# Contrast adjustment of 48 image planes: the first tile of four planes is split into tiles of one, one and two planes

## The chip, the cores and the metric

The kernel runs on one NeuronCore of a Trainium2 chip. The metric is the device time of one execution in microseconds (us); lower is better. A core has a tensor engine (PE), a vector engine (DVE), a scalar engine (ACT), a GpSimd engine (POOL) and a sync engine (SP). Each runs its own instruction stream in order, and they wait for each other through semaphores. Data moves between DRAM and the on-chip memory through 16 DMA engines that serve two queues here: one filled by SP (loads), one filled by ACT (stores).

## The reference

```python
def setup_inputs():
    batch, c, h, w = 16, 3, 512, 512
    return {
        "x": np.random.rand(batch, c, h, w).astype(np.float32),
        "factor": np.float32(1.5),
    }

def reference(x: np.ndarray, factor: np.float32) -> np.ndarray:
    mean = np.mean(x, axis=(2, 3), keepdims=True)
    return np.clip(mean + factor * (x - mean), 0, 1).astype(np.float32)
```

There are 16 x 3 = 48 planes of 512 x 512 float32 numbers, 1 MB each; this document calls one plane an image. Each image needs its own mean before any of its numbers can be written. 50.33 MB are read and 50.33 MB are written. Written out, the result is clip(factor * x + (1 - factor) * mean, 0, 1).

## The kernel before

The images lie one behind the other in DRAM. A tile is 128 partitions by 8192 numbers (a row of 32 KB in each partition), 4 MB, which is exactly four images with 32 partitions each. There are 12 tiles, and a ring of six tile slots in on-chip memory, in which each tile is loaded, changed in place, and stored from.

For each tile `compute` (L78) does this:

1. DVE adds up columns 0 to 4351 of each partition (L81), while ACT adds up columns 4352 to 8191 through an activation with an accumulator (L84). The split is the constant SUM.
2. PE multiplies the two columns of partial sums with a 128 x 128 block matrix `blockw` (L86 for ACT's sums, L87 for DVE's). Its blocks of 32 x 32 hold (1 - factor) / (512 * 512), so that every partition of an image gets (1 - factor) * mean in `bias`. POOL writes the matrix at the start (L61, L63).
3. DVE computes factor * x + bias in place (L91), then clips with max and min in place (L94).
4. ACT issues the store (L101), behind DVE's clip.

The order of the work is written by hand. ACT runs its sum of tile t+1 behind the store of tile t in its stream, so it can't begin that sum before DVE has clipped tile t. SP issues the loads (L76): first the first 2048 columns of tile 0 (8 KB rows), then the other 6144 columns of tile 0 (24 KB rows), then tile 1, then tiles 2 and 3 in one DMA, then tiles 4 and 5 in one DMA. This fills the ring. From then on the load of tile t + 6 stands behind compute of tile t, and SP waits for the store of tile t before it issues it, since it goes to the same slot. Tile 0 is also finished and stored in two parts, of 2048 and of 6144 columns (FIRST, L89): two stores, with 8 KB and with 24 KB rows. A load of two tiles counts as landed only when both are there.

A DMA of 128 rows is cut into packets, one for each row, so that each of the 16 engines moves 8 packets of it.

Of the kernel before, what the change touches and what calls it, by code (L numbers as in the profile page):

```python
# [1 line left out]

# [4 lines left out]


P = 128  # L10
ROW = 8192
BUFS = 6
SHORT = 2048
FIRST = (SHORT, ROW - SHORT)
SUM = 4352


@with_exitstack
def kernel(
    ctx: ExitStack,  # L20
    tc: tile.TileContext,
    x: bass.AP,
    factor: float,
    out: bass.AP,
):

    nc = tc.nc
    f32 = mybir.dt.float32  # L30
    Alu = mybir.AluOpType
    Act = mybir.ActivationFunctionType

    B, C, H, W = x.shape
    n_img, n_pix = B * C, H * W
    ppi = n_pix // ROW
    per_tile = P // ppi
    n_tiles = n_img // per_tile
    assert ppi * ROW == n_pix and per_tile * n_tiles == n_img

    factor = float(factor)
    wconst = (1.0 - factor) / float(n_pix)

    x_f = x.rearrange("b c h w -> (b c h w)")
    out_f = out.rearrange("b c h w -> (b c h w)")

    def dram(ap, t, c0=0, c1=ROW):
        return bass.AP(tensor=ap.tensor, offset=t * P * ROW + c0, ap=[[ROW, P], [1, c1 - c0]])

    consts = ctx.enter_context(tc.tile_pool(name="consts", bufs=1))  # L50
    xpool = ctx.enter_context(tc.tile_pool(name="xpool", bufs=1))
    small = ctx.enter_context(tc.tile_pool(name="small", bufs=1))
    psum = ctx.enter_context(tc.tile_pool(name="psum", bufs=1, space=bass.MemoryType.PSUM))


    sums = small.tile([P, 2 * n_tiles], f32, name="sums")
    junk = small.tile([P, ROW - SUM], f32, name="junk")
    bias = psum.tile([P, n_tiles], f32, name="bias")

    blockw = consts.tile([P, P], f32, name="blockw")  # L60
    nc.gpsimd.memset(blockw, 0.0)  # L61
    for a in range(0, P, ppi):
        nc.gpsimd.memset(blockw[a : a + ppi, a : a + ppi], wconst)  # L63


    ring = xpool.tile([P, BUFS, ROW], f32, name="ring")

    def load(t, c0=0, c1=ROW, n=1):

        b = t % BUFS  # L70
        src = bass.AP(
            tensor=x_f.tensor,
            offset=t * P * ROW + c0,
            ap=[[ROW, P], [P * ROW, n], [1, c1 - c0]],
        )
        nc.sync.dma_start(out=ring[:, b : b + n, c0:c1], in_=src)  # L76

    def compute(t):  # L78
        xt = ring[:, t % BUFS, :]
        own = sums[:, 2 * t : 2 * t + 2]  # L80
        nc.vector.tensor_reduce(  # L81
            out=own[:, 0:1], in_=xt[:, 0:SUM], axis=mybir.AxisListType.X, op=Alu.add
        )
        nc.scalar.activation(out=junk, in_=xt[:, SUM:ROW], func=Act.Copy, accum_out=own[:, 1:2])  # L84
        shift = bias[:, t : t + 1]
        nc.tensor.matmul(shift, blockw, own[:, 1:2], start=True, stop=False)  # L86
        nc.tensor.matmul(shift, blockw, own[:, 0:1], start=False, stop=True)  # L87
        c = 0
        for n in FIRST if t == 0 else [ROW]:  # L89
            part = xt[:, c : c + n]  # L90
            nc.vector.tensor_scalar(  # L91
                out=part, in0=part, scalar1=factor, scalar2=shift, op0=Alu.mult, op1=Alu.add
            )
            nc.vector.tensor_scalar(  # L94
                out=part, in0=part, scalar1=0.0, scalar2=1.0, op0=Alu.max, op1=Alu.min
            )
            store(t, c, c + n)
            c += n

    def store(t, c0, c1):  # L100
        nc.scalar.dma_start(out=dram(out_f, t, c0, c1), in_=ring[:, t % BUFS, c0:c1])  # L101

    with tc.manual_schedule():
        load(0, c1=SHORT)
        load(0, c0=SHORT)
        load(1)
        load(2, n=2)
        load(4, n=2)
        for t in range(n_tiles):
            compute(t)  # L110
            if t + BUFS < n_tiles:
                load(t + BUFS)


# [1 line left out]
_INS = ['x', 'factor']  # L116
_OUTS = [((16, 3, 512, 512), 'float32')]

_NUMBERS = {'factor': 1.5}


# [26 lines left out]
```

## Time and profile before

| What | us |
|---|---|
| median of 3 runs | 239.27 (239.14 to 239.34) |
| span of the profiled execution, first to last instruction | 237.3 |
| DVE busy | 163.1 (69%) |
| ACT busy | 43.2 (18%) |
| PE busy | 14.1 (6%) |
| POOL busy | 0.9 |
| DVE sum of a tile, L81, 12 times | 4.683 each |
| ACT sum of a tile, L84, 12 times | 3.403 each |
| DVE scale and shift, 8192 columns, L91, 11 times | 4.491 each |
| DVE clip, 8192 columns, L94, 11 times | 4.427 each |
| DVE scale and shift, 2048 columns, L91, once | 1.291 |
| DVE clip, 2048 columns, L94, once | 1.227 |
| DVE idle in front of L81, waiting for loads | 45.7 in total |
| first load (1 MB), issue to landing | 4.8 |
| store of a tile, issue to landing, median | 35.8 |

The profile is of one execution; its own time on record is its span, and the runs' median includes what lies around it. The profile's page lists busy time by engine, cuts the span into 40 equal slices of about 5.9 us with the busy share of each engine and of the DMA engines in tenths, gives packets and bytes of each DMA queue with the time that their packets took as a share of all 16 engines, follows the chain of waits back from the end, and groups instructions by line. Other views give busy times and DMA traffic in chosen windows, the instructions in order of time, and the waits of each engine. q1 is the queue of SP's loads, q10 the queue of ACT's stores. In a window, packets are counted where they begin, so a share can come out somewhat over 100%.

DVE begins its first sum at 12.96 us, when the whole of tile 0 has landed. The first store is issued at 20.91 us, the last at 218.17 us. SP issues its first load at 0.74 us.

### The profile page before, as it was taken

What the parts mean: (1) busy time and instruction counts of PE and PEld (TensorE: products, weight loads), DVE (VectorE), ACT (ScalarE), POOL (GpSimd) and SP (SyncE); (2) the same over time, 40 slices, a digit from 0 to 9 for tenths busy, and PEclk for the clock granted to TensorE, in tenths of its full rate; (3) what the DMA queues carried; (4) which work ended last, traced back from release to release, by engine and by line L of the source; (5) the groups of instructions that cost most, each with busy time, mean ns of one, the idle gap of its engine ahead of it and who ended that gap; (6) DMA issues with size and microseconds to landing.
All of it is one profiled execution on the core that took longest, in us unless ns stands there. A gap on an engine that the chain in (4) does not pass through costs nothing.

```text
span 237.3 us, 285 instructions
## 1 busy us (share of the span) xinstructions
PE 14.1 (6%) x48; PEld 12.0 (5%) x48; DVE 163.1 (69%) x38; ACT 43.2 (18%) x25; POOL 0.9 (0%) x9
## 2 busy tenths in 40 slices
PE   0010010001010001010010100100100100010000
PEld 0010010001010001010010100100100100010000
DVE  0079989048989328999989898891892795687000
ACT  2050230041050023050320504101400500500000
POOL 1000000000000000000000000000000000000000
DMA  7999999999999999999999999999999999999996
GB/s 297 410 442 442 421 442 359 456 439 441 442 436 414 403 431 442 442 442 442 436 442 436 414 409 425 442 442 442 442 436 442 436 420 403 425 442 442 442 442 265
DMA packets 3712, 100.66 MB, mean 424 GB/s; under 512 B 384, under 2 KB 384, under 8 KB 384
## 3 DMA queue, kind: packets, MB, share of 16 engines
q1 hardware_dynamic: 1840, 50.33, 49.7%
q10 hardware_dynamic: 1872, 50.33, 49.2%
HBM read 50.33 MB, written 50.33 MB: 424 GB/s over the span
## 4 chain that ended last, share of the span: by engine, by line
DMA 57%; DVE 29%; another core or an unknown queue 3%; PE 1%; SPq 1%; issue 0%; DVEq 0%
DMA ring<-in_x_dram 41%; DMA out_dram<-ring 16%; DVE sums L81 10%; DVE ring L91 9%; DVE ring L94 9%; PE bias L87 1%; SPq L76 1%; DVEq L91 0%
## 5 line engine op out<-in xcount | busy, mean ns | idle before, releaser
L81 DVE TENSOR_REDUCE sums<-ring 128x1 f32<-128x4352 f32 x12 | 56.2, 4683 | 45.7 <-DMA ring<-in_x_dram 45.7
L84 ACT ACTIVATE junk<-ring 128x3840 f32<-128x3840 f32 x12 | 40.8, 3403 | 163.3 <-DMA ring<-in_x_dram 107.5
L91 DVE TENSOR_SCALAR ring<-ring,bias 128x8192 f32<-128x8192 f32 (+2 forms) x13 | 54.1, 4163 | 8.9 <-PE bias L87 7.4
L94 DVE TENSOR_SCALAR ring<-ring 128x8192 f32<-128x8192 f32 (+2 forms) x13 | 53.3, 4099 | 0.4
L86 PE MATMUL bias<-sums,blockw 128*128 128x1 f32 x24 | 7.0, 361 | 190.8 <-ACT junk L84 190.8
L86 PEld LDWEIGHTS bias<-sums,blockw 128*128 128x128 f32 x24 | 6.0, 312 | 191.7 <-ACT junk L84 175.2
L87 PE MATMUL bias<-sums,blockw 128*128 128x1 f32 x24 | 7.0, 363 | 4.3 <-DVE sums L81 3.9
L87 PEld LDWEIGHTS bias<-sums,blockw 128*128 128x128 f32 x24 | 6.0, 311 | 5.3 <-DVE sums L81 5.0
L84 ACT ACTIVATION_READ_ACCUMULATOR junk<-ring 128x1 f32 x12 | 2.2, 186 | 0.0
L84 ACT ACT_TABLE_LOAD x1 | 1.3, 1283 | 0.7 <-PEq L129 0.7
L63 POOL MEMSET blockw<- 32x32 f32 x4 | 0.5, 117 | 0.2
L61 POOL MEMSET blockw<- 128x128 f32 x1 | 0.2, 204 | 0.3 <-POOLq L129 0.3
L129 POOL MEMSET const-bfloat16-1.0<- 128x1 bf16 x1 | 0.1, 111 | 0.0
L129 POOL MEMSET const-uint8-127<- 128x1 uint8 x1 | 0.1, 111 | 0.0
L129 POOL MEMSET const-float32-1.0<- 128x1 f32 x1 | 0.1, 108 | 0.0
L129 POOL MEMSET const-float32-0.0<- 128x1 f32 x1 | 0.1, 103 | 0.2 <-issue 0.2
## 6 DMA issues: line engine op xcount, KB each, us to landing
out_dram<-ring ACTq DMA_DIRECT2D x11, 4096.0 KB, 35.8
ring<-in_x_dram SPq DMA_DIRECT2D x7, 4096.0 KB, 49.7
ring<-in_x_dram SPq DMA_DIRECT2D x2, 8192.0 KB, 66.7
ring<-in_x_dram SPq DMA_DIRECT2D x1, 3072.0 KB, 11.7
out_dram<-ring ACTq DMA_DIRECT2D x1, 3072.0 KB, 28.2
ring<-in_x_dram SPq DMA_DIRECT2D x1, 1024.0 KB, 4.8
out_dram<-ring ACTq DMA_DIRECT2D x1, 1024.0 KB, 17.5
```

The costliest lines, as they stand in the source:

```text
L61: nc.gpsimd.memset(blockw, 0.0)
L63: nc.gpsimd.memset(blockw[a : a + ppi, a : a + ppi], wconst)
L76: nc.sync.dma_start(out=ring[:, b : b + n, c0:c1], in_=src)
L81: nc.vector.tensor_reduce(out=own[:, 0:1], in_=xt[:, 0:SUM], axis=mybir.AxisListType.X, op=Alu.add)
L84: nc.scalar.activation(out=junk, in_=xt[:, SUM:ROW], func=Act.Copy, accum_out=own[:, 1:2])
L86: nc.tensor.matmul(shift, blockw, own[:, 1:2], start=True, stop=False)
L87: nc.tensor.matmul(shift, blockw, own[:, 0:1], start=False, stop=True)
L91: nc.vector.tensor_scalar(out=part, in0=part, scalar1=factor, scalar2=shift, op0=Alu.mult, op1=Alu.add)
L94: nc.vector.tensor_scalar(out=part, in0=part, scalar1=0.0, scalar2=1.0, op0=Alu.max, op1=Alu.min)
L129: nc = _bacc.Bacc("TRN2", target_bir_lowering=False, num_devices=1)
```

## The change

The first tile of four images becomes three tiles: image 0 alone, image 1 alone, and images 2 and 3 together. A tile of n images now has 128 / n partitions for each image, so that a tile of one image has 128 rows of 2048 numbers (8 KB), a tile of two has rows of 16 KB, and a tile of four has rows of 32 KB as before. The other eleven tiles hold the same images in the same rows as before. There are 14 tiles:

- Each tile is one load (alone, or two tiles in one DMA) and one store; the splits of tile 0 by columns are gone.
- SP's first loads are tile 0 (1 MB), tile 1 (1 MB), tile 2 (2 MB), tile 3 (4 MB), then 4 and 5 in one DMA, then 6 and 7 in one DMA. These are 24 images and fill the ring, which holds as much as before, now as one flat row of columns in each partition.
- Tiles 0, 1 and 2 together lie where tile 8 goes, so the load of tile 8 stands behind compute of tile 2 and waits for three stores.
- DVE's share of each sum becomes 36/64 (4608 of 8192 columns, 1152 of 2048) in place of 4352 of 8192; ACT adds up the rest.
- There is a block matrix for each tile size (one block of 128 x 128, two of 64 x 64, four of 32 x 32).

```diff
-ROW = 8192
-BUFS = 6
-SHORT = 2048
-FIRST = (SHORT, ROW - SHORT)
-SUM = 4352
+IMG = 2048
+SLOTS = 6
+
+TILES = (1, 1, 2) + (4,) * 11
+
+SHARE = 36
...
+    first = [sum(TILES[:t]) for t in range(n_tiles)]
+    columns = SLOTS * 4 * IMG
...
+    block = {}
+    for n in sorted(set(TILES)):
+        rows = P // n
+        block[n] = m = consts.tile([P, P], f32, name=f"block{n}")
+        nc.gpsimd.memset(m, 0.0 if n > 1 else wconst)
+        for a in range(0, P, rows) if n > 1 else ():
+            nc.gpsimd.memset(m[a : a + rows, a : a + rows], wconst)
 
-    ring = xpool.tile([P, BUFS, ROW], f32, name="ring")
+    ring = xpool.tile([P, columns], f32, name="ring")
...
+    def dram(ap, t, n=1):
+        row = TILES[t] * IMG
+        return bass.AP(
+            tensor=ap.tensor, offset=first[t] * n_pix, ap=[[row, P], [P * row, n], [1, row]]
         )
-        nc.sync.dma_start(out=ring[:, b : b + n, c0:c1], in_=src)
+
+    def load(t, n=1):
+        a = first[t] * IMG % columns
+        row = TILES[t] * IMG
+        dst = ring[:, a : a + n * row].rearrange("p (n r) -> p n r", r=row)
+        nc.sync.dma_start(out=dst, in_=dram(x_f, t, n))
 
     def compute(t):
-        xt = ring[:, t % BUFS, :]
+        xt = cols(t)
+        row = TILES[t] * IMG
+        vec = row * SHARE // 64
...
-        c = 0
-        for n in FIRST if t == 0 else [ROW]:
-            part = xt[:, c : c + n]
-            nc.vector.tensor_scalar(
-                out=part, in0=part, scalar1=factor, scalar2=shift, op0=Alu.mult, op1=Alu.add
-            )
-            nc.vector.tensor_scalar(
-                out=part, in0=part, scalar1=0.0, scalar2=1.0, op0=Alu.max, op1=Alu.min
-            )
-            store(t, c, c + n)
-            c += n
...
+        nc.vector.tensor_scalar(
+            out=xt, in0=xt, scalar1=factor, scalar2=shift, op0=Alu.mult, op1=Alu.add
+        )
+        nc.vector.tensor_scalar(
+            out=xt, in0=xt, scalar1=0.0, scalar2=1.0, op0=Alu.max, op1=Alu.min
+        )
+        nc.scalar.dma_start(
+            out=dram(out_f, t), in_=xt.rearrange("p (n r) -> p n r", n=1)
+        )
 
     with tc.manual_schedule():
-        load(0, c1=SHORT)
-        load(0, c0=SHORT)
+        load(0)
         load(1)
-        load(2, n=2)
+        load(2)
+        load(3)
         load(4, n=2)
+        load(6, n=2)
         for t in range(n_tiles):
             compute(t)
-            if t + BUFS < n_tiles:
-                load(t + BUFS)
+            if t >= 2 and t + SLOTS < n_tiles:
+                load(t + SLOTS)
```

Here `cols(t)` is the part of the ring that holds tile t: columns `first[t] * IMG % columns` on, `TILES[t] * IMG` of them.

## The prediction

> **What bounds the kernel now.** I read the chain of waits first, then the 40 slices, then the DMA queues window by window, and the engines last.
>
> ```profile
> DMA 57%; DVE 29%; another core or an unknown queue 3%; PE 1%; SPq 1%; issue 0%; DVEq 0%
> ...
> DMA  7999999999999999999999999999999999999996
> GB/s 297 410 442 442 421 442 359 456 439 441 442 436 414 403 431 442 442 442 442 436 442 436 414 409 425 442 442 442 442 436 442 436 420 403 425 442 442 442 442 265
> ...
> q1 hardware_dynamic: 1840, 50.33, 49.7%
> q10 hardware_dynamic: 1872, 50.33, 49.2%
> ```
>
> The chain names VectorE (DVE) for 29%, which invites the reader to shorten the compute. The DMA row says otherwise: every slice but the first and the last is at 9 or more. The two queues (q1 loads, q10 stores) together hold the 16 engines for 49.7 + 49.2 = 98.9% of the 237.3 us span, 234.7 us; some 2.0 us pass before the first load moves data, and about 1 us after the last packet. No compute is seen through that wall. Cut into stretches:
>
> ```profile
> 2.00:12.00 10.00, 0.00 (x0) 0.00 (x0) 0.00 (x0) 0.02 (x1) 0.00 (x0) 1.00 1.01 426
> 12.00:24.00 12.00, 1.15 (x4) 1.01 (x4) 10.33 (x4) 3.50 (x2) 0.00 (x0) 1.00 0.99 426
> ...
> 60.00:120.00 60.00, 3.52 (x12) 3.00 (x12) 49.39 (x12) 13.75 (x7) 0.00 (x0) 1.00 1.01 437
> ...
> 203.00:235.00 32.00, 1.18 (x4) 1.01 (x4) 13.60 (x3) 3.50 (x2) 0.00 (x0) 1.00 1.00 433
> ```
>
> The columns are window, length, PE, weight load, DVE, ACT, POOL busy, clock, DMA share, GB/s. The DMA share is 1.0 with loads alone (2 to 12), with both queues (60 to 120), and with stores alone (203 to 235, when no load is left). So the time is **the price of all packets in a row**, and the change can move it only by changing packets' prices or by letting the engines run dry.
>
> **Prices of packets,** from the queues' packets and shares in chosen windows:
>
> ```profile
> DMA packets 161, 3.31 MB, mean 414 GB/s; under 512 B 0, under 2 KB 0, under 8 KB 0
> q1 hardware_dynamic: 81, 2.65, 76.9%
> q10 hardware_dynamic: 80, 0.66, 19.3%
> ...
> q1 hardware_dynamic: 48, 1.57, 52.3%
> q10 hardware_dynamic: 52, 1.28, 42.3%
> ...
> q10 hardware_dynamic: 471, 13.86, 100.3%
> ```
>
> First, 28 to 36 us: 80 store packets of 8 KB take 19.3% of 16 x 8 us, 0.309 us each; 81 loads of 32 KB beside them take 1.215. Each engine serves one packet of each queue in turn, whatever their sizes (81 against 80). Second, 41 to 48: 24 KB stores, 42.3% of 112 us over 52, 0.911. Third, 203 to 235: 423 packets of 32 KB (48 more carry only a semaphore), 1.214. So 8, 24 and 32 KB cost 0.309, 0.911, 1.213; a 16 KB packet isn't in the trace; the line between its neighbours gives (0.309 + 0.911) / 2 = 0.610, with bounds of half a 32 KB packet (0.607) and two of 8 KB (0.618).
>
> One thing costs more. The load queue holds 0.5% of the span (1.2 us) more than the store queue for the same bytes. Two places make most of it:
>
> ```profile
> q1 hardware_dynamic: 67, 2.13, 86.7%
> ...
> q1 hardware_dynamic: 32, 1.05, 58.2%
> ```
>
> From 22 to 28 us, where the 8 KB store begins, 65 loads of 32 KB take 83.2 engine-us, 1.281 each: (1.281 - 1.213) x 65 / 16 = 0.27 us. From 37 to 42, where the 24 KB store follows it, 32 loads take 1.455 each: 0.48 us. I call this a stretched start. The first 32 KB store behind them, around 57, shows none (from 55 to 61 the shares again fit 1.21). The remaining 1.2 - 0.75 = 0.45 us is the first load finding idle engines.
>
> **The change, part by part.** Tiles 3 to 13 of the new kernel are tiles 1 to 11 of the old one: same bytes, same 32 KB rows, same single and paired loads. What differs is the first 4 MB, and a share.
>
> *Packets.* Each engine gets 8 packets of a 128-row transfer. Old first tile, per direction: 8 x 0.309 + 8 x 0.911 = 9.76 us. New: 16 x 0.309 + 8 x 0.610 = 9.82. Twice the difference: **+0.13 us** (+0.1 to +0.25 by the bounds of the 16 KB price).
>
> *Starts.* Now two store transfers shorter than 32 KB rows (0.27 + 0.48 = 0.75), then three: 8, 8, 16 KB. Bounds for each: 0, as for the 32 KB store, to 0.48. For the two 8 KB starts I take the row of their own size, 0.27; for 16 KB, between 8 and 24, 0.375: 0.92 in all, **+0.17 us**. Range 0 to 1.44, so -0.75 to +0.69.
>
> *First load.* 128 packets of 8 KB on idle engines before and after; only the DRAM rows now lie end to end. I keep its 0.45 us (bounds 0 and twice that).
>
> *One more load and one more store.* The Trainium skill, DMA: Bandwidth & Descriptors (Anatomy of one DMA, and Bandwidth), speaks against this: about 2.0 us fixed for each DMA, measured on the GpSimd path, and a rule to batch. In line, two more would make +4 us, 243.3, an estimate from that page alone. The trace shows no such gap: where a 1 MB load is followed by the 3 MB one and then by 4 MB, the share from 2 to 12 us stays at 1.01, so I put nothing in. SP spends one more issue (0.42 us, by the chain); its last issue moves from about 2.7 to 3.3 us, while the four loads ahead of it keep the engines until about 23 us or later. Without that cover it would cost 0.42.
>
> *Earlier compute.* The first load lands at 0.74 + 4.8 = 5.5 us, now a whole image; DVE begins there, not at 12.96. First compute: reduce of 1152 columns about 1.35 (between 4.69 x 1152 / 4352 = 1.24 and that plus a fixed part of some 0.2), 0.75 of matmuls, 1.29 + 1.23 for 2048 columns: the store is issued at about 10.1, not 20.9. Second: 14.7. Third (16 KB rows): 8.0 more, 22.7. It buys nothing as long as the engines are busy anyway.
>
> *Share.* DVE's part of a sum goes from 4352 to 4608 of 8192 columns, 4.69 x 256 / 4352 = +0.28 us per big tile; ACT gives back 0.23. Eleven times 0.28 is hidden by the 45.7 us in which DVE waits for loads; uncovered it is 3.0.
>
> *Extra instructions.* Three block matrices in place of one (9 memsets for 5, some 0.7 us more of POOL, done near 2.5 us, needed near 7), two more passes of four matmuls, ACT sums and reads: all before 23 us, behind loads that are moving.
>
> *Waits.* The reload of the first slots (image 24 on) waits for three stores instead of two; behind it on SP wait only later reloads. By turns: stores start about 4.6 us after the first issue as they do now (20.9 to about 25.5), so at 14.7; 8 turns of 0.309 + 1.213 = 12.2, again 12.2, then 8 of 1.82 = 14.6: the third lands at 53.7, like the 54 to 56 us of now. The loads of the first four images end near 2.0 + 0.45 + 9.82 = 12.3, so by 53.7 loads have moved 24 turns plus about 2 packets of 32 KB, 3.2 big tiles beyond those images. The paired load of tiles 6 and 7 runs until about 86, so the reload is 30 us early.
>
> *The end.*
>
> ```profile
> 198.81 0.34 ACTq L101 DMA_DIRECT2D out_dram<-ring  x1
> ...
> 218.17 0.34 ACTq L101 DMA_DIRECT2D out_dram<-ring  x1
> ```
>
> The last store is issued at 218.17 but needs the engines for only 8 x 1.213 = 9.7 us before about 236.3: it stands in line for 8.5 us. The loads' lead over the stores decides this. It is now 3.3 tiles when the first four images are stored, then 3.2: 0.1 x 9.7 = 1 us less, and 0.28 for the share: some 7 us of cover stay.
>
> **Sum.** 237.3 + 0.13 + 0.17 = 237.6 of span; the runs' median of 239.27 lies 2.0 above the span, which I carry: 239.57, **239.6 us**, +0.13%. A measurement of this kernel can tell about 0.2%, 0.48 us, from no change.
>
> **Rivals.**
> *Dearer starts (slower).* The stretch belongs to every store that follows a smaller or equal small one while big loads run: 3 x 0.48 = 1.44, +0.69 + 0.13: **240.1**. For it: the second start cost more than the first. Against: the third cost nothing. It decides the sign from a mean of (0.75 + 0.48 - 0.13) / 3 = 0.37 us a start, close to what I take, so it is the strongest rival.
> *Starts without stretch (faster).* If the stretch came from storing 8 and 24 KB pieces of 32 KB rows, it goes, since every store now covers one unbroken piece of DRAM: -0.75 + 0.13: **238.65**; with a smoother first load, 238.2. Nothing in the trace parts this from the first.
> *Bare end (slower).* If stores that start earlier ate the loads' lead until each store began the moment it was ready, only the 0.77 tile that half-rate stores move in 14.9 us would be left in line, 7.5 us of work against 14.9 of compute: 7.4 us of idle engines, **246.7**. It decides once the lead falls by over 0.8 tile. Against: small store packets take turns with 32 KB loads, which preserves the lead.
> *Compute counts.* If the chain's DVE share were real, 12.96 - 5.5 = 7.5 us would go: **231.8**. Against: the DMA rows; the packets alone need 234.
> *The reload waits for more than its three stores* (a tracker that sees the flat ring as one piece): hidden for 30 us; no time of its own.
>
> **Chances.** Forecast (239.0 to 239.75 by itself) 0.56; dearer starts 0.24; no stretch 0.15; bare end 0.03; compute counts 0.02. Slower 0.24 + 0.03 = 0.27; within 0.2% 0.56; faster 0.15 + 0.02 = 0.17. The range takes in both bounds of the starts: 238.6 to 240.2; the last two rivals stay out.
>
> **What would show it.** Right: slices at 9 throughout, the two queues' shares summing to 234.5 to 235.5 us, no idle between the last load's landing and the last packet, the last store issued near 218, a load queue again about 0.5% above the store queue, DVE starting near 5.5, the first reload issued near 54. Wrong: a slice under 9 after the first (dry engines), a 16 KB packet far from 0.61, a load queue at twice its surplus (dearer starts) or level with the stores (no stretch), or the last store reaching the engines as soon as it is issued (bare end).

## The result, and the profile after

The changed kernel takes 239.76 us (median of 19 runs, 239.53 to 239.94) against 239.27: ratio 1.0021, 95% interval 1.0015 to 1.0027. The forecast was 239.6, range 238.6 to 240.2. The rise of 0.49 us sits on the 0.2% line that the prediction drew. The span of the profiled execution is 237.6 us, which is the forecast's own sum. Its parts are not the forecast's parts, and that is what the rest is about.

First the page after: slices and queues.

```profile
DMA  6999999999999999999999999999999999999996
...
q1 hardware_dynamic: 1984, 50.33, 49.6%
q10 hardware_dynamic: 2016, 50.33, 49.1%
```

The engines are full throughout, as before. The queues take 98.7% of 237.6 us, 234.5 us, against 98.9% of 237.3, 234.7. **In this execution the stream of packets has not become longer.** By stretches (window, length, PE, weight load, DVE, ACT, POOL, clock, DMA share, GB/s):

```profile
60.00:120.00 60.00, 3.52 (x12) 3.01 (x12) 50.53 (x12) 12.59 (x7) 0.00 (x0) 1.00 1.01 437
203.00:235.00 32.00, 1.18 (x4) 1.00 (x4) 13.87 (x3) 3.28 (x2) 0.00 (x0) 1.00 1.01 436
```

DVE works 1.14 us more between 60 and 120 (its larger share of the sums), and nothing follows from it. In order of time:

```profile
5.64 1.35 DVE L88 TENSOR_REDUCE sums<-ring 128x1 f32<-128x1152 f32 x1 [5.64 <-DMA ring<-in_x_dram]
...
54.91 0.34 SPq L81 DMA_DIRECT2D ring<-in_x_dram  x1
...
218.43 0.34 ACTq L103 DMA_DIRECT2D out_dram<-ring  x1
```

Compute starts 7.3 us earlier, the first reload goes out at 54.91, the last store at 218.43. All three were foretold within 1.5 us, and the 7.3 us bought nothing.

So the profiled 0.36 us must lie outside the packets. The trace's record of every packet places it: the last data packet ends 236.05 us after the span's start before, and 236.04 after. What comes behind it, the tail from here on, lasts 1.22 us before and 1.60 after. **The time was lost behind the last packet.** The instructions there are put down to one line, L143 before and L148 after. At the end each engine runs a drain, which raises a semaphore that POOL waits for; POOL then releases all engines through another. This happens twice, and I call it the barrier. Columns: how often, shortest/median/longest in ns, start of the first and the last. Before:

```profile
L143 SPq EVENT_SEMAPHORE  x8: 17/28/10929, 173.4 to 237.2; - x8
...
L143 ACTq DRAIN  x2: 8/80/152, 218.5 to 236.8; - x2
```

After:

```profile
L148 SPq EVENT_SEMAPHORE  x8: 17/28/32665, 153.4 to 237.6; - x8
...
L148 ACTq DRAIN  x2: 118/136/153, 218.8 to 237.3; - x2
```

Two things differ. SP now stands for 32.7 us in a single wait instead of passing its waits one by one as stores land. And ACT's last drain takes 118 ns instead of 8 and begins 0.41 us after the release in front of it, not 0.09. SP's last records, one by one (us from the span's start; S[n] is a semaphore):

```
before: 217.10 S[108],S[104]   226.80 S[109],S[105]   236.46 S[110],S[103]   236.53 drain
after:  203.73 S[106],S[101] (held 32.67 us, to 236.39)
        236.43 S[107],S[100]   236.49 S[108],S[103]   236.55 S[109],S[105]   236.61 S[110],S[102]   236.68 drain
```

Eight semaphores serve all DMAs in turn (S[100], S[101], S[102] or S[104], then S[106] to S[110]; the others in these records are raised by engines). SP's last six waits have a fixed order: a single one, S[106] with S[101], S[107] with S[100], then S[108], S[109] and S[110]. Before, the last store of 24 DMAs has S[110], the last in that order; the waits ahead of it were passed while earlier stores landed. After, there are 26 DMAs, the last store has S[101], and four waits of 0.06 us stand behind it though their semaphores were full long before (by 226.7 us at the latest). From the last packet to SP's drain it is 0.48 us before and 0.64 after; from there to the end 0.74 and 0.96, and the second step is ACT's drain.

The first step holds a part that varies from one execution to the next: the last store's semaphore is full 0.33 to 0.46 us behind the last packet. From that moment to SP's drain it is 0.08 us before and 0.30 after, so the four waits cost 0.22.

### The profile page after: what moved, and what is told of

The parts are those of the page before. It is cut to its first block, busy times and chain, and to the rows that moved or that the text cites. A ratio compares the mean times of both kernels' runs of the same rounds, so it can differ in the third digit from the quotient of the medians.

```text
span 237.6 us, 322 instructions
## 1 busy us (share of the span) xinstructions
PE 15.9 (7%) x56; PEld 13.8 (6%) x56; DVE 166.9 (70%) x42; ACT 41.3 (17%) x29; POOL 1.4 (1%) x13
## 5 line engine op out<-in xcount | busy, mean ns | idle before, releaser
L88 DVE TENSOR_REDUCE sums<-ring 128x1 f32<-128x4608 f32 (+2 forms) x14 | 59.7, 4264 | 39.4 <-DMA ring<-in_x_dram 39.4
L91 ACT ACTIVATE junk<-ring 128x3584 f32<-128x3584 f32 (+2 forms) x14 | 38.7, 2763 | 165.1 <-DMA ring<-in_x_dram 99.2
L95 PE MATMUL bias<-sums,block 128*128 128x1 f32 x28 | 8.1, 359 | 184.6 <-ACT junk L91 184.6
L95 PEld LDWEIGHTS bias<-sums,block 128*128 128x128 f32 x28 | 7.0, 311 | 185.6 <-ACT junk L91 164.0
L96 PE MATMUL bias<-sums,block 128*128 128x1 f32 x28 | 8.2, 360 | 8.9 <-DVE sums L88 8.9
L96 PEld LDWEIGHTS bias<-sums,block 128*128 128x128 f32 x28 | 7.2, 317 | 9.9 <-DVE sums L88 9.9
L63 POOL MEMSET block<- 32x32 f32 (+1 forms) x6 | 0.8, 126 | 0.2
L61 POOL MEMSET block<- 128x128 f32 x3 | 0.5, 204 | 0.3 <-POOLq L134 0.3
```

The lines of the kernel that those rows point to most:

```text
L61: nc.gpsimd.memset(m, 0.0 if n > 1 else wconst)
L63: nc.gpsimd.memset(m[a : a + rows, a : a + rows], wconst)
L88: nc.vector.tensor_reduce(out=own[:, 0:1], in_=xt[:, 0:vec], axis=mybir.AxisListType.X, op=Alu.add)
L91: nc.scalar.activation(out=junk[:, 0 : row - vec], in_=xt[:, vec:row], func=Act.Copy, accum_out=own[:, 1:2])
L95: nc.tensor.matmul(shift, block[TILES[t]], own[:, 1:2], start=True, stop=False)
L96: nc.tensor.matmul(shift, block[TILES[t]], own[:, 0:1], start=False, stop=True)
```

## The experiments

The **end theory**: the cost is those waits and that drain, set by the number of DMAs and by where ACT's instruction stream ends. The **starts theory** is the prediction's own: small stores stretch the loads beside them. All kernels below were timed against the kernel before on the same chip (239.18 to 239.22 there).

**1. Before with 26 DMAs.**

```diff
-        load(2, n=2)
-        load(4, n=2)
+        load(2)
+        load(3)
+        load(4)
+        load(5)
```

> The kernel before, with tiles 2, 3, 4 and 5 loaded one by one instead of in pairs: 26 DMAs like the changed kernel instead of 24, the same packets and the same stores. End theory (the change costs its time after the last packet: SP still has waits on other DMA counters to pass behind the one that the last store releases, because the counters are handed out in turns of eight): the last packet ends at 236.1 as before, the tail behind it grows by about 0.18 us, time 239.4 to 239.5. Starts theory (the cost lies in small store packets): no change, 239.27. A fixed 2 us for each further DMA: 243.

241.13 us, ratio 1.0096 (1.0067 to 1.0126). The tail is 1.39, 0.17 more than before with four waits behind the last store, as the end theory had it. But something that no theory expected is ten times as large, and so none of the three times forecast came true: the last packet ends at 237.97.

```profile
235.00:236.00 1.00, 0.00 (x0) 0.00 (x0) 0.00 (x0) 0.00 (x0) 0.00 (x0) 1.00 0.23 98
236.00:237.00 1.00, 0.00 (x0) 0.00 (x0) 0.00 (x0) 0.00 (x0) 0.00 (x0) 1.00 0.15 66
```

In the kernel before, the share is 0.01 and 0.00 in these two windows. Here three of the 16 engines still move packets (the last of them end at 236.92, 237.76 and 237.97), while the others are done by 235.9. Experiment 12 returns to it.

**2. After with 24 DMAs.**

```diff
-        load(0)
-        load(1)
+        load(0, n=2)
         load(2)
-        load(3)
-        load(4, n=2)
+        load(3, n=3)
         load(6, n=2)
```

> The changed kernel with tiles 0 and 1 loaded in one DMA and tiles 3, 4 and 5 in one DMA: 24 DMAs like the kernel before, the same 14 stores in the same sizes. End theory: SP's waits behind the last store are gone again, which takes 0.18 us of the 0.36 that the profiled tail grew; 239.5 if ACT's late drain (0.2 us) stays, 239.3 if it goes too. Starts theory: the three small stores are all there, so as the changed kernel, 239.7 to 239.8.

239.28 us, ratio 1.0004 (0.9995 to 1.0013): the whole rise is gone with all three small stores in place.

```profile
L146 SPq EVENT_SEMAPHORE  x8: 17/28/28, 183.3 to 237.3; - x8
...
L146 ACTq DRAIN  x2: 8/80/152, 210.1 to 236.9; - x2
```

No long wait on SP and a prompt drain on ACT; tail 1.18.

**3. Before with the larger DVE share** (`SUM = 4608`).

> The kernel before with DVE's part of each sum at 4608 of 8192 columns, as in the changed kernel. Both theories: the 0.28 us more a tile is hidden by DVE's wait for loads, 239.27 within 0.1. A rival in which DVE's chain sets the end: 11 x 0.28 = 3 us more, 242.3.

239.05 us, ratio 0.9999 (0.999 to 1.0009). The share costs nothing that this run can tell, which is 0.1%.

**4. Before with tile 0 in one piece.**

```diff
-        load(0, c1=SHORT)
-        load(0, c0=SHORT)
+        load(0)
...
-        for n in FIRST if t == 0 else [ROW]:
+        for n in [ROW]:
```

> The kernel before with tile 0 loaded as one 4 MB DMA and stored as one: no packets of 8 or 24 KB are left, 22 DMAs. Stretched starts belong to small stores: 0.75 us of stretches and 0.11 us of packet prices go, two waits at the end are added (0.12), 238.5. Stretch belongs to the first store that meets the loads, whatever its size: 0.27 stays, 238.8. If an early first store were worth something, this kernel's first store comes 6.5 us later and the time rises above 239.27.

239.59 us, ratio 1.002 (1.001 to 1.003): a miss for the starts theory in all its forms. No data packet is smaller than 32 KB, and yet, from 28 to 34 us, where the first store begins:

```profile
q1 hardware_dynamic: 58, 1.90, 86.6%
q10 hardware_dynamic: 16, 0.52, 20.2%
```

58 loads take 86.6% of 96 us, 1.433 each: (1.433 - 1.213) x 58 / 16 = 0.80 us, in one go. Of the 0.4 us rise about 0.1 is the tail (22 DMAs, two waits behind the last store, 1.32). The rest is ahead of the last packet (236.47), and its cause stays open: the last branch of the expectation forecast a rise, but the first load is another here too, so the run doesn't show that the later first store is the reason. In the changed kernel a first store 10.4 us earlier gained nothing.

**5. After, unaltered, for a second profile.**

> The changed kernel once more, unaltered, for a second profile of its end. End theory: last packet again within 0.2 us of 236.1, SP again with four waits behind the one that the last store releases (about 0.06 us each), tail near 1.6 us against 1.2 of the kernel before; 239.7 to 239.8. If ACT's late last drain (0.2 us) is chance, it is gone here and the tail is 1.4. Starts theory: load queue's surplus over the store queue clearly above the 1.2 us of before.

239.76 us, ratio 1.0022 (1.0011 to 1.0032). Last packet 236.27, four waits, the drain late again (0.4 us behind the barrier, 118 ns), tail 1.61. It is not chance. The load queue's surplus, summed packet by packet, is 1.40 us; in the first profile it was 1.08, in the kernel before 1.24. So two profiles of one kernel differ by more than the starts theory needs, and the stream of packets too ended 0.23 us later here than in the first.

**6 and 7. The two halves of experiment 2,** 25 DMAs each: `load(0, n=2)` alone, and `load(3, n=3)` alone.

> One half of the 24-DMA run: only tiles 0 and 1 are loaded in one DMA, 25 DMAs. End theory: the last store gets the first of the eight counters, SP's waits on later ones stay behind it, tail 1.35 to 1.7, time 239.5 to 239.9. A rival (merging the first loads was what helped in the 24-DMA run): 239.3 with a tail of 1.2.

> The other half: only tiles 3, 4 and 5 are loaded in one DMA, 25 DMAs. End theory: as its sister run, tail 1.35 to 1.7, time 239.5 to 239.9. A rival (the longer lead of the loads, since compute waits for three tiles, was what helped in the 24-DMA run): 239.3 with a tail of 1.2.

239.43 (1.0003 to 1.002) and 239.57 us (1.0008 to 1.0026), tails 1.31 and 1.33 with three waits behind the last store, which has S[100]. ACT's drain is prompt in both. Neither merge alone is what helped in experiment 2. The intervals overlap with that run's, so the weight is on the profiles.

**8. Before with 25 DMAs:** `load(4, n=2)` as two loads.

> The kernel before with only the pair of tiles 4 and 5 split into two loads, 25 DMAs. End theory: tail 1.35 to 1.7 instead of 1.22, the packets as before, 239.4 to 239.8. If splitting pairs is what set three of the 16 engines back in the 26-DMA run of the kernel before, some engine falls behind by over 0.5 us here too and the time is above 240.

239.43 us, ratio 1.0011 (1.0002 to 1.002), three waits, tail 1.34, last packet 236.15. No engine falls behind.

**9 and 10. After with one and with four further ACT instructions.**

```diff
         load(6, n=2)
+        for _ in range(4):
+            nc.scalar.activation(out=junk[:, 0:1], in_=block[1][:, 0:1], func=Act.Copy)
```

> The changed kernel with one further ACT instruction, a copy of one column while ACT waits for the first image. If ACT's late last drain (0.3 us later than in other runs) comes from where its instruction stream ends, for instance at the edge of a block of instructions that is fetched, then one more instruction moves that edge to the instruction before the drain, still in the end: tail about 1.6, or 1.4 if it falls out of the end. If the late drain has another cause (the four waits of SP), the tail stays at 1.60 with the drain late as before.

> The changed kernel with four further ACT instructions of the same kind. If the place in ACT's instruction stream counts, the stall has moved ahead of the last store's landing, where ACT waits anyway: last drain prompt, tail about 1.4 with SP's four waits still there, time 239.5. If not, tail 1.60 and 239.76.

239.65 (1.0006 to 1.0025) and 239.56 us (1.0003 to 1.0022), tails 1.44 and 1.40. With one more instruction:

```profile
L150 ACTq DRAIN  x2: 8/62/117, 219.3 to 237.2; - x2
...
q14 instruction: 1, 0.01, 0.0%
```

The long drain (117 ns) is now ACT's first, at 219.3, while the last stores are still moving; the last one takes 8 ns again. And a queue that is not on the changed kernel's page has appeared: q14, an 8 KB packet of instructions, at 223.6 us. With four more, that packet comes at 207.8 and both drains are ordinary. The changed kernel's own trace has such a packet too, behind its span, at 237.94:

```profile
237.00:238.00 1.00, 0.00 (x0) 0.00 (x0) 0.00 (x0) 0.00 (x0) 0.00 (x0) 1.00 0.02 8
```

So the late drain belongs to a place in ACT's instruction stream, and a few instructions more push it under the stores.

**11. Before with seven further ACT instructions.**

> The kernel before with seven further ACT instructions, so that the trace should hold 65 of ACT as for the changed kernel, not 58. If the place in the stream counts, and if the count in the trace is the one that matters, the last drain comes late here and the tail is 1.42 (1.22 + 0.2) without any further wait on SP; 239.4. If it does not, 1.22 and 239.2.

239.25 us, ratio 1.0001 (0.9992 to 1.0011), tail 1.18. The trace holds 67 instructions of ACT, two more than meant, so the last drain is prompt. But the first one is late: it starts 0.69 us behind the start of the last store's issue (0.38 in the kernel before) and takes 130 ns, and the instruction packet follows at 223.5 us.

That gives the count. The last drain of the changed kernel, the first drain here and the first drain in experiment 9 are all the 64th of ACT's instructions that the trace holds. In experiment 10 the 64th is the last sum, and it starts 0.38 us behind the wait in front of it instead of 0.06. In these four traces and in experiment 5 the 64th comes 0.31 to 0.33 us late. In experiments 6 and 7 it is ACT's very last wait, which hides all but 0.02 to 0.03 us; in experiment 12 it stands in a wait of 15.5 us. The other traces have 54 to 62 instructions of ACT, and in none of them is a drain late.

**12. After with both pairs split,** 28 DMAs: tiles 4, 5, 6 and 7 loaded one by one.

> The changed kernel with both pairs (4 and 5, 6 and 7) loaded tile by tile, 28 DMAs. End theory alone: the last store gets the fourth counter, four waits behind it or one less, tail 1.35 to 1.6, 239.5 to 239.8. If splitting both pairs sets some engines back, as in the kernel before with 26 DMAs, the last packet comes 1 to 2 us later: 240.5 to 242.

243.04 us, ratio 1.0158 (1.0141 to 1.0175). The tail is 1.40 with four waits, but the last packet ends at 239.68. From 130 to 136 us:

```profile
q1 hardware_dynamic: 48, 1.57, 67.1%
q10 hardware_dynamic: 46, 0.98, 38.1%
```

48 loads take 67.1% of 96 us, 1.342 each, in the middle of the run; in the kernel before the same window has 48 loads at 60.6%, 1.212:

```profile
q1 hardware_dynamic: 48, 1.57, 60.6%
```

In experiment 1 it has 48 at 61.1%, 1.222, so there the middle of the run is hardly slower. Loads over the whole span hold 1.3% of 241.1 us more than stores, 3.1 us against 1.2:

```profile
q1 hardware_dynamic: 2016, 50.33, 49.8%
q10 hardware_dynamic: 2016, 50.33, 48.5%
```

All together:

| Kernel | DMAs | Waits behind the last store | Last packet ends | Tail | Median us |
|---|---|---|---|---|---|
| before | 24 | 0 | 236.05 | 1.22 | 239.27 |
| 2: after, 24 DMAs | 24 | 0 | 236.20 | 1.18 | 239.28 |
| 3: before, share | 24 | 0 | 236.13 | 1.29 | 239.05 |
| 11: before, ACT + 7 | 24 | 0 | 236.21 | 1.18 | 239.25 |
| 4: before, one piece | 22 | 2 | 236.47 | 1.32 | 239.59 |
| 6: after, 25 DMAs | 25 | 3 | 236.13 | 1.31 | 239.43 |
| 7: after, 25 DMAs | 25 | 3 | 236.09 | 1.33 | 239.57 |
| 8: before, 25 DMAs | 25 | 3 | 236.15 | 1.34 | 239.43 |
| 1: before, 26 DMAs | 26 | 4 | 237.97 | 1.39 | 241.13 |
| 10: after, ACT + 4 | 26 | 4 | 236.10 | 1.40 | 239.56 |
| 9: after, ACT + 1 | 26 | 4 | 236.21 | 1.44 | 239.65 |
| 12: after, pairs split | 28 | 4 | 239.68 | 1.40 | 243.04 |
| after | 26 | 4, drain late | 236.04 | 1.60 | 239.76 |
| 5: after again | 26 | 4, drain late | 236.27 | 1.61 | 239.76 |

The tail follows the waits (1.18 to 1.29 with none, 1.31 to 1.34 with two or three, 1.39 to 1.44 with four), and only the changed kernel as it is pays the late drain on top. The two parts come out cleaner when they are counted from the moment at which the last store's semaphore is full: to SP's drain it is 0.08 us with no wait behind it, 0.20 with two, 0.24 with three and 0.30 to 0.33 with four; from there to the end 0.74 to 0.75 in every run, and 0.96 in the two profiles of the changed kernel.

## Why the prediction was right, and where it was not

**Bound and cover: right.** The time is the price of the packets in a row. Earlier compute, the share, the further block matrices and the reload that waits for three stores cost and gain nothing that shows (experiment 3 for the share; for the rest the DMA share of 1.0 in the stretches above). The last store still stood in line: issued at 218.43, it needed the engines for 9.7 us before 236.0.

**Packets, +0.13: right.** The 16 KB packet takes 0.611 us in the trace after, where the line between its neighbours gave 0.610.

**Starts, +0.17: wrong.** Four windows of the changed kernel, 12 to 16, 20 to 25, 38 to 42 and 48 to 52 us, show the loads beside the beginnings of the three small stores and beside the third one's last packets:

```profile
q1 hardware_dynamic: 64, 1.57, 96.6%
...
q1 hardware_dynamic: 62, 1.51, 72.9%
...
q1 hardware_dynamic: 42, 1.38, 83.8%
...
q1 hardware_dynamic: 48, 1.05, 63.7%
```

They hold 48, 46, 42 and 32 loads of 32 KB (from the bytes; the rest are semaphores of 0.009 us), 1.285, 1.265, 1.277 and 1.270 us each, an excess of 0.22 + 0.15 + 0.17 + 0.11 = 0.65 us. The prediction summed 0.92 by giving each start its own price. The runs show no price per start: 0.75 us with two small stores, 0.65 with three, 0.80 with one big one. Over whole traces, the 32 KB loads exceed 1.213 us by 0.82 to 0.87 us in all for the kernel before and experiments 3, 8 and 11, and by 0.47 to 0.80 for the changed kernel and experiments 2, 5, 6, 7, 9 and 10 (0.68 and 0.80 in the two profiles of the changed kernel). So the sum was about the same, however many stores it was spread over, and the term was between -0.14 and -0.02 by these two, not +0.17. The rivals built on it fall with it: dearer starts, since three cost no more than two; no stretch, since a store that covers one unbroken piece of DRAM stretches the loads as much.

**One more load and one more store, at nothing: wrong, and this is the step that failed.** I looked for their cost where they are issued and where they run, found it hidden, and carried the time around the packets ("some 2.0 us pass before the first load moves data, and about 1 us after the last packet") unchanged. The cost is behind the last packet: 0.22 us of waits and 0.21 us of ACT's drain, less 0.06 by which the last store's semaphore followed its last packet sooner in this profile. That is 0.37 of the 0.49 us; the remaining 0.1 is within what one profile differs from the next (last packets at 236.04 and 236.27). That 24 DMAs bring the time back to 239.28 was shown by experiment 2, that the waits go with the number of DMAs in both kernels by 1, 4, 6, 7, 8 and 12, and that the drain goes with the number of ACT's instructions by 9, 10 and 11. The drain's part thus falls to the extra instructions as well, which the prediction put at nothing because they run before 23 us: they bring ACT from 58 instructions in the trace to 65, and its last drain to the 64th place.

The forecast of 239.6 thus came out near 239.76 since 0.2 to 0.3 too much in the starts stood against 0.37 missing at the end. The sum was right by luck in two of its terms.

The rule that was weighed, a fixed 2 us for each DMA (the Trainium skill, DMA: Bandwidth & Descriptors, Anatomy of one DMA), is for the GpSimd path. By an estimate from it, experiment 8 would take 241.2; with one DMA more than the kernel before (239.18 beside it) it measured 239.43, and about half of the rise is in the tail.

**Open:** why the loads stretch when stores join; why the first load's 0.45 us varies (in the two profiles of the changed kernel, the 8 KB packets of its loads cost 0.44 and 0.64 us in all beyond a price of 0.309 each); why ACT's 64th instruction is late; and what sets engines back when both pairs are split. For the last: the last store of experiment 12 was issued at 224.49 and its 9.7 us ended at 239.68, so it stood in line, and DVE was not the bound. One pair split sets no engine back (experiment 8). No version here is faster than the kernel before beyond the noise.

## What to carry to other kernels

When a kernel keeps its DMA engines full from start to end, rearranging work around the stream changes only what stands before the first packet and behind the last, so read those two ends from the trace instruction by instruction before costing a further DMA at nothing. Ask which semaphore the last transfer releases and how many waits are still queued behind it: here two DMAs more, hidden themselves, cost 0.22 us that way. A term that is read off one or two places (0.27 and 0.48 for two starts) is not yet a price per event; one kernel with a single event would have shown that the sum stays the same.

## What the runs showed of the hardware

- In these traces the 64th of ACT's instructions starts 0.31 to 0.33 us late wherever no longer wait covers it. In the changed kernel that is the last drain; it took 118 ns and held the final barrier by 0.21 us, in both profiles. With one instruction more, it is the first drain, 18 us earlier and hidden. An 8 KB packet of instructions starts 0.6 us behind the late instruction when the engines are idle, and 3.6 to 4.5 us behind it while stores are moving, so the instruction does not wait for that packet to land. The Trainium skill, Runtime: NRT & Kernel Launch (Instruction fetch mechanics), says that crossing a block of 16 KiB of instructions costs one bump of a DMA queue's tail, mostly hidden. The packet behind the delay fits that, and the changed kernel would be the case in which it is not hidden; that the delay is this bump is not shown.
- Splitting both paired loads, with no other edit, took 1.9 us in the kernel before and 3.3 in the changed one. In both, engines end at different times (235.5 to 236.1 us in the kernel before; three of them at 236.9 to 238.0 in experiment 1; all between 236.8 and 239.7 in experiment 12). Loads that run at 1.342 instead of 1.212 us in the middle of the run are seen in experiment 12 alone.
- Packets take turns one to one between the two queues whatever their size (81 of 32 KB against 80 of 8 KB from 28 to 36 us, before and after), so a store with 8 KB rows beside 32 KB loads progresses slowly and takes little: the last load ended at 203.4 us in both kernels, although the stores began 10 us earlier.
